# A projection's tile asks for the next two weight units, where it asked for the next one

## The chip, the core and the metric

The kernel runs on one core of a Trainium2 chip. A core has five engines that run side by side, each with its own queue, which it works through strictly in order: TensorE (PE, matrix products), VectorE (DVE), ScalarE (ACT), GpSimd (POOL) and SyncE (SP, which here only starts DMA transfers). An instruction that has to wait for another engine keeps back all that stands behind it on its own engine. The metric is the device time of one launch, in microseconds (us).

## What is computed

Two transformer blocks on 256 tokens of width 1024, in fp32. The first has an RWKV7 recurrence beside stick-breaking attention, then a feed-forward part. The second has a token mixer of two recurrences side by side and a mixture of 64 experts:

```python
def token_mixer(h, w_in, ...):
    proj = jnp.einsum('btd,de->bte', h, w_in)
    qkv = causal_short_conv(proj[..., :qkv_w], conv_w)
    ...
    oA = gated_delta_chunked(qA, kA, vA, g_log, beta)      # "gdn": a triangular solve per chunk of 64
    oA = rms_norm_2(oA, gdn_norm_w) * jax.nn.silu(gateA)
    ...
    oB = hgrn2_chunked(qB, kB, iB, logf)                   # "hgrn"
    oB = rms_norm_2(oB, hg_norm_w) * jax.nn.silu(gateB)
    return jnp.einsum('bte,ed->btd', jnp.concatenate([oA, oB], -1), w_out)
x = x + g1 * token_mixer(...)
x = x + g2 * moe(...)                                      # 64 experts, 8 for each token
```

## The kernel before, in words

**Weight units.** All projections outside the experts read one packed weight array, cut in 168 units of eight 128x128 tiles. `unit(u)` (L270) brings a unit in: SP loads it into one of three `raw` buffers (L274); ACT copies it, rounded to TensorE's fast fp32 format, into `whi` (L324); and DVE, or POOL for the thirty units listed in `POOLU`, writes the rest `wlo = raw - whi` (L325). `whi` and `wlo` have three buffers each. A tile then takes three matmuls (L330 to L332, L352 to L358): whi by the high part of x, whi by its low part, wlo by the high part; a unit is 24 matmuls. Most outputs (128 columns of a projection) take eight tiles, but since a block of twelve tiles stands early in the array, each output of the mixer takes the second half of one unit and the first half of the next.

**Asking ahead.** The line that the change is about is in `wt`, which every tile of a projection goes through:

```python
        hi, lo = self.unit(u)
        for v in range(u + 1, min(u + AHEAD + 1, -(-self.ntiles // UNIT) if u > 2 else 0)):
            self.unit(v)
```

So with `AHEAD = 1` the tile of unit u writes into the program the load and the split of unit u+1, if they are not there yet. Where these instructions then stand on each engine is settled by a scheduler, which orders the program by its own estimates; the strings `FIRST` and `MIXER` say in what order the program's streams (generators) are advanced.

**The mixer of the second block.** Its streams: `proj_fiq` (L1260 to L1281) makes hgrn's inputs: cumulated log decays by scans (L1270), queries (L1274), values (ACT copies, L1279). `proj_qv` makes gdn's queries and values, through `conv`: ACT takes the projection out of PSUM (L1130), DVE adds three shifted copies (L1133). `proj_gates2` (L1302) makes the gates. `gdn` builds the chunks' triangular matrices (masks on POOL, L1217 and L1218; product on DVE, L1223) and has `inverse` invert them: SP writes them to DRAM and back in another layout (L411, L414); `base_inverse` (L381) eliminates column by column on DVE, 31 pairs of a product (L393) and a subtraction (L394) on 32 partitions; ACT transposes (L395); SP writes the result to DRAM (`da`, L425) and reads it back (L429, L432); then PE goes on with products of small blocks (L403). `hgrn` works in two halves of 128 tokens: POOL copies inputs (L1409 to L1413), seven levels each take DVE differences (L1423, L1424), an exponential on ACT (L306), products on DVE and POOL (L1426, L1427), matmuls (L1429) and a masked copy on DVE (L1435). `second_mix` then makes the output projection, and the router and the experts follow, whose weights SP starts to load (L1729) behind the mixer's last `raw` loads.

Units 131 to 162 belong to this mixer: the first half of unit 143, whose `wlo` POOL makes, ends `proj_fiq`; its second half and the first of unit 144 make `proj_qv`'s first output; the gates end in the middle of unit 159, and the output projection begins there.

Of the kernel before, what the change touches and what calls it, by code (L numbers as in the profile page):

```python
# [40 lines left out]
UNIT = 8  # L41
RAW = 3
MIXER = 'kkkffkfkkfkfffffffkfqkkqqqqqqqqddghhfdhhgdhhgghhhhhhdhhhghh'
AHEAD = 1
POOLU = (17, 18, 26, 29, 36, 42, 46, 51, 65, 68, 69, 72, 94, 105, 109, 111, 112, 115, 116, 117, 119, 120, 121, 140, 143, 145, 149, 151, 158, 161)
NG = 12
FIRST = 'iiivvvivvvvvvsssssssswsssswgwxxwxxwxxxxwgwwwxgxxgooggggg'
# [162 lines left out]
class Ker:  # L210
# [74 lines left out]
    def wt(self, block, i):  # L285
        i += self.off[block]
        u = i // UNIT
# [3 lines that stand above are left out]
# [1889 lines left out]
```

## Time and profile before

| what | us |
| --- | --- |
| median of 3 runs | 1167.34 |
| lowest and highest of them | 1165.89, 1170.15 |
| the profiled execution's own time | 1175.33 |
| its span, from first to last instruction | 1173.5 |
| TensorE busy in it | 1086.6 |
| VectorE busy in it | 682.1 |
| ScalarE busy in it | 436.8 |
| GpSimd busy in it | 243.0 |

The rows come from the profiled execution, which took 8.0 us longer than the median of the runs; of its own time 1.83 us lie outside the span. Busy time is time in which an engine carries out instructions; the rest it waits. The stages follow each other in the trace: first block to about 360 us, its feed-forward part and the start of the second block to 556, the mixer from 556 to 732, router and experts from there to the end.

### The profile page before, as it was taken

To read this page: it belongs to the slowest core of one execution; us is meant where nothing else is said; L and a number is where in the kernel's file an instruction comes from. 1 tells how busy PE (TensorE), PEld (TensorE's weight loads), DVE (VectorE), ACT (ScalarE), POOL (GpSimd) and SP (SyncE) were. 2 spreads that over 40 slices of the span, in tenths; PEclk is the share of its full clock that TensorE was granted. 3 is DMA by queue.
4 is the path that set the end of the run, shared out by engine and by line. 5 is a ranking of instruction groups with operands and counts; after the bars stand their busy time and mean duration, and the time that the engine had idled before them with its cause. 6 is when DMAs were issued, how large, how long until landed. Compare 5 with 4: busy or idle time off the path is not lost.

```text
span 1173.5 us, 20361 instructions
## 1 busy us (share of the span) xinstructions
PE 1086.6 (93%) x8038; PEld 831.6 (71%) x8038; DVE 682.1 (58%) x1211; ACT 436.8 (37%) x707; POOL 243.0 (21%) x245
## 2 busy tenths in 40 slices
PE   5989899999989999988988999899999999999994
PEld 4889787789979999877988889773444444444441
DVE  5598633346678888877799888522233333333333
ACT  5744433365454444335854645411111111111112
POOL 1261102023312000486472131410000000000000
PEclk9899969999989999998999999799999999999998
DMA  5455511024558898864443504959999999999993
GB/s 174 141 145 176 177 55 37 1 86 166 179 198 298 314 341 302 306 232 145 148 146 127 176 28 174 415 182 344 418 413 392 419 419 419 399 419 418 420 418 139
DMA packets 67495, 290.69 MB, mean 248 GB/s; under 512 B 15984, under 2 KB 17136, under 8 KB 46912
## 3 DMA queue, kind: packets, MB, share of 16 engines
q1 hardware_dynamic: 66528, 287.93, 65.5%
q8 instruction: 66, 1.08, 0.4%
q10 hardware_dynamic: 864, 1.38, 0.3%
q14 instruction: 37, 0.30, 0.1%
HBM read 285.77 MB, written 3.51 MB: 247 GB/s over the span
## 4 chain that ended last, share of the span: by engine, by line
PE 45%; DMA 16%; DVE 11%; issue 4%; ACT 4%; POOL 3%; SPq 0%; POOLq 0%; ACTq 0%; DVEq 0%
DMA er<-in_E_dram 10%; PE bank L1880 10%; PE bank L1908 5%; PE p_b L357 3%; PE p_b L358 3%; PE p_b L352 3%; DMA wada<-in_W_ada_dram 3%; PE acc L1777 3%; PE bank L1840 3%; DMA xa<-in_E_dram 3%; DVE wada L1086 2%; DVE wlo L325 2%; PE p_b L787 2%; ACT k L306 2%; PE p_b L332 2%
## 5 line engine op out<-in xcount | busy, mean ns | idle before, releaser
L324 ACT ACTIVATE whi<-raw 128x1024 fp32r<-128x1024 f32 x168 | 175.5, 1055 | 102.7 <-PE p_b L331 37.0
L325 DVE TENSOR_TENSOR wlo<-raw,whi 128x1024 fp32r<-128x1024 f32 x138 | 178.4, 1299 | 59.5 <-ACT whi L324 55.4
L358 PE MATMUL p_b<-k,wlo 128*128 128x256 f32 x608 | 175.7, 290 | 4.9 <-DVE wlo L325 3.0
L352 PE MATMUL p_b<-k,whi 128*128 128x256 f32 x608 | 176.1, 290 | 3.5 <-ACT k L324 2.3
L357 PE MATMUL p_b<-k,whi 128*128 128x256 f32 x608 | 176.1, 290 | 2.3 <-DVE k L325 2.3
L332 PE MATMUL p_b<-k,wlo 128*128 128x256 f32 (+2 forms) x496 | 144.6, 296 | 13.1 <-DVE wlo L325 9.0
L330 PE MATMUL p_b<-k,whi 128*128 128x256 f32 (+2 forms) x496 | 146.8, 300 | 9.3 <-ACT k L324 4.1
L331 PE MATMUL p_b<-k,whi 128*128 128x256 f32 (+2 forms) x432 | 126.8, 296 | 0.3 <-DVE k L1114 0.3
L358 PEld LDWEIGHTS p_b<-k,wlo 128*128 128x128 f32 x608 | 118.6, 195 | 8.3 <-DVE wlo L325 4.0
L352 PEld LDWEIGHTS p_b<-k,whi 128*128 128x128 f32 x608 | 118.8, 196 | 5.1 <-ACT k L324 2.4
L325 POOL TENSOR_TENSOR wlo<-raw,whi 128x1024 fp32r<-128x1024 f32 x30 | 81.6, 2723 | 196.7 <-ACT whi L324 136.5
L357 PEld LDWEIGHTS p_b<-k,whi 128*128 128x128 f32 x608 | 118.8, 196 | 3.8 <-DVE k L325 2.8
L332 PEld LDWEIGHTS p_b<-k,wlo 128*128 128x128 f32 (+1 forms) x496 | 97.1, 198 | 15.8 <-DVE wlo L325 10.9
L330 PEld LDWEIGHTS p_b<-k,whi 128*128 128x128 f32 (+1 forms) x496 | 97.4, 198 | 14.6 <-ACT k L324 5.1
L1880 PE MATMUL bank<-er,x 128*32 128x512 f32 (+2 forms) x464 | 91.9, 612 | 2.6 <-DMA er<-in_E_dram 2.5
L1908 PE MATMUL bank<-er,k 128*32 128x512 f32 (+2 forms) x488 | 89.9, 595 | 2.6 <-DMA er<-in_E_dram 1.4
L1880 PE MATMUL bank<-er,h 128*32 128x512 f32 (+2 forms) x488 | 87.5, 595 | 0.0
L1828 POOL TENSOR_TENSOR k<-k,masks 128x128 f32<-128x128 f32 (+3 forms) x44 | 17.3, 423 | 335.7 <-DVE y L325 310.8
L331 PEld LDWEIGHTS p_b<-k,whi 128*128 128x128 f32 (+1 forms) x432 | 85.7, 199 | 0.8 <-DVE k L1114 0.6
L1086 DVE SCALAR_TENSOR_TENSOR wada<-wada,crow 128x1024 f32<-128x1024 f32 x48 | 70.9, 1484 | 21.7 <-DMA wada<-in_W_ada_dram 21.6
L1885 ACT ACTIVATE k<-bank 128x256 f32<-128x256 f32 x24 | 9.2, 384 | 195.7 <-PE bank L1880 195.7
L1886 DVE SCALAR_TENSOR_TENSOR k<-k,gs,bank 128x256 f32<-128x256 f32 x24 | 11.5, 481 | 101.9 <-ACT k L1885 101.9
(476 smaller groups left out, 2043.5 us busy)
## 6 DMA issues: line engine op xcount, KB each, us to landing
er<-in_E_dram SPq DMA_DIRECT2D x132, 1024.0 KB, 17.7
raw<-in_W_dram SPq DMA_DIRECT2D x168, 512.0 KB, 3.9
wada<-in_W_ada_dram SPq DMA_DIRECT2D x48, 512.0 KB, 5.5
xa<-in_E_dram SPq DMA_DIRECT2D x24, 1024.0 KB, 12.5
xa<-in_Sh_dram SPq DMA_DIRECT2D x2, 1024.0 KB, 8.3
k<-in_xT_dram SPq DMA_DIRECT2D x4, 272.0 KB, 4.7
dl<-x SPq DMA_DIRECT2D x1, 1024.0 KB
x<-in_xT_dram SPq DMA_DIRECT2D x1, 1024.0 KB
```

What stands on the lines that cost most here:

```text
L324: ins = self.nc.scalar.activation(hi, src, AF.Copy)
L325: (engine or self.nc.vector).tensor_tensor(lo, src, hi.bitcast(F32), op=OP.subtract)
L330: mm(out, w[0], x[0], start=start, stop=False)
L331: mm(out, w[0], x[1], start=False, stop=False)
L332: mm(out, w[1], x[0], start=False, stop=stop)
L352: a = mm(p[:, i], w[0], v[0], start=(n == 0), stop=False, **kw)
L357: mm(p[:, i], w[0], v[1], start=False, stop=False, **kw)
L358: mm(p[:, i], w[1], v[0], start=False, stop=last, **kw)
L1086: nc.vector.scalar_tensor_tensor(w, w, 1.0, c, op0=OP.mult, op1=OP.mult, accum_out=self.mod[:, o:o + 1])
L1777: self.nc.tensor.matmul(self.acc[t], w, x, start=t not in self.started, stop=False, skip_group_check=True)
L1880: mm(ph[t], X[:, k, i * 128 + t.start:i * 128 + t.stop], u[:, kk * 512:kk * 512 + 512], start=(k == 0), stop=(k == KD - 1), skip_group_che ...
L1908: nc.tensor.matmul(py[t], q.H[:, k, t], u[:, k * 1024 + c * 512:k * 1024 + c * 512 + 512], start=(k == 0), stop=(k == 1), skip_group_check ...
```

## The change

One constant is changed; nothing is computed in another way.

```diff
-AHEAD = 1
+AHEAD = 2
```

A tile of unit u now has the units u+1 and u+2 brought in. Each engine carries out the same instructions as before; what changes is the place of some of them, in the first block from unit 10 to 18 (44 to 90 us of the trace) and in the second block's mixer from unit 131 to 162 (556 to 720 us). Between these, units 19 to 130, each engine's order is the same as before.

On VectorE, where the mixer's triangular inverse begins. Before:

```order
L1426 TENSOR_TENSOR h_7056<-h_7056,h_7039 128x8x32
L1424 TENSOR_TENSOR h_7102<-h_7037 128x32x8
L1426 TENSOR_TENSOR h_7090<-h_7090,h_7039 128x16x16
L1426 TENSOR_TENSOR h_7102<-h_7102,h_7039 128x32x8
L393 TENSOR_TENSOR kt<-gate 32x31
L394 TENSOR_TENSOR gate<-gate,kt 32x31
```

and with the change:

```order
L325 TENSOR_TENSOR wlo<-raw,whi 128x1024
L1426 TENSOR_TENSOR h_7062<-h_7062,h_7045 128x8x32
L1426 TENSOR_TENSOR h_7096<-h_7096,h_7045 128x16x16
L1423 TENSOR_TENSOR h_7108<-h_7043 128x32x8
L1424 TENSOR_TENSOR h_7108<-h_7043 128x32x8
L1426 TENSOR_TENSOR h_7108<-h_7108,h_7045 128x32x8
L1133 SCALAR_TENSOR_TENSOR k_6553<-p_b_6555,cols,k_6553 128x255
L1133 SCALAR_TENSOR_TENSOR k_6553<-p_b_6555,cols,k_6553 128x254
L1133 SCALAR_TENSOR_TENSOR k_6553<-p_b_6555,cols,k_6553 128x253
L393 TENSOR_TENSOR kt<-gate 32x31
L394 TENSOR_TENSOR gate<-gate,kt 32x31
```

The `wlo` in the second piece is unit 144's, which stood inside the inverse before; the three L1133, which work on the product of units 143 and 144 (`p_b_6555`, `proj_qv`'s first output), stood behind the inverse's ninth pair and now stand ahead of its first.

On ScalarE, at the same place (the L1279 are `proj_fiq`'s last outputs, of which the last ends in unit 143; L1130 is `proj_qv`'s first). Before:

```order
L306 ACTIVATE h_7102<-h_7102 128x512
L1279 ACTIVATE k_5915<-p_b_6397 128x256
L1279 ACTIVATE k_5915<-p_b_6515 128x256
L324 ACTIVATE whi<-raw 128x1024 x3
L1130 ACTIVATE k_6547<-p_b_6549,cols 128x256
```

and with the change:

```order
L324 ACTIVATE whi<-raw 128x1024
L306 ACTIVATE h_7062<-h_7062 128x512
L1279 ACTIVATE k_5921<-p_b_6403 128x256
L306 ACTIVATE h_7096<-h_7096 128x512
L306 ACTIVATE h_7108<-h_7108 128x512
L1279 ACTIVATE k_5921<-p_b_6521 128x256
L1130 ACTIVATE k_6553<-p_b_6555,cols 128x256
```

Unit 144's `whi`, the first of the three behind the L1279 before, now stands ahead of three of hgrn's exponentials.

On SyncE, where the inverse's result is sent out. Before:

```order
L274 DMA raw<-in_W_dram 128x1024 x16
L425 DMA da_6505<-gate 32x1024 x2
L274 DMA raw<-in_W_dram 128x1024
L432 DMA gate<-da_6505 32x8x32
L429 DMA k_6429<-da_6505 32x8x32 x2
```

and with the change:

```order
L274 DMA raw<-in_W_dram 128x1024 x17
L425 DMA da_6511<-gate 32x1024 x2
L274 DMA raw<-in_W_dram 128x1024
L432 DMA gate<-da_6511 32x8x32
L429 DMA k_6435<-da_6511 32x8x32 x2
```

Since the loads' run begins one unit later than before (unit 145 instead of 144), it now ends with unit 161 instead of 159: units 160 and 161 are asked for ahead of `da`, and unit 162 in place of unit 160 between its writing and its reading. On POOL, the first of hgrn's copies (L1409) now stands ahead of the second pair of gdn's masks (L1217, L1218) instead of behind it.

## Rows read from the trace of the kernel before

**Rows 1.** The page's head: span, and busy time of each engine.
```profile
span 1173.5 us, 20361 instructions
PE 1086.6 (93%) x8038; PEld 831.6 (71%) x8038; DVE 682.1 (58%) x1211; ACT 436.8 (37%) x707; POOL 243.0 (21%) x245
```

**Rows 2.** The page's groups of `wlo`: count, busy us, mean ns, idle before.
```profile
L325 DVE TENSOR_TENSOR wlo<-raw,whi 128x1024 fp32r<-128x1024 f32 x138 | 178.4, 1299 | 59.5 <-ACT whi L324 55.4
L325 POOL TENSOR_TENSOR wlo<-raw,whi 128x1024 fp32r<-128x1024 f32 x30 | 81.6, 2723 | 196.7 <-ACT whi L324 136.5
```

**Rows 3.** Busy time by stage; the first line names the columns.
```profile
core 0: us, PE busy (x) PEld busy (x) DVE busy (x) ACT busy (x) POOL busy (x), PEclk, DMA share, GB/s
60.00:88.00 28.00, 24.80 (x205) 23.07 (x204) 27.30 (x37) 11.83 (x16) 17.73 (x14) 1.00 0.57 152
...
400.00:440.00 40.00, 39.77 (x335) 39.57 (x334) 36.37 (x55) 18.23 (x28) 2.40 (x1) 1.00 0.89 324
560.00:600.00 40.00, 36.86 (x297) 35.11 (x297) 31.96 (x63) 34.16 (x71) 20.53 (x22) 1.00 0.45 146
600.00:660.00 60.00, 51.23 (x396) 49.66 (x395) 58.98 (x121) 31.12 (x44) 19.65 (x11) 0.94 0.44 137
660.00:680.00 20.00, 19.54 (x219) 17.83 (x220) 15.21 (x21) 13.88 (x21) 6.80 (x5) 1.00 0.50 149
```

**Rows 4.** PE's waits in 556 to 730: us in total, times, longest.
```profile
PE p_b L332 <- DVE wlo L325: 4.1, 4, 2.5
PE p_b L332 <- POOL wlo L325: 4.0, 2, 2.4
PE p_b L358 <- DVE wlo L325: 1.7, 1, 1.7
```

**Rows 5.** DVE's timeline round the inverse: start, us, line; in brackets idle before.
```profile
604.18 0.42 DVE L1426 TENSOR_TENSOR h<-h,h 128x256 f32<-128x256 f32 x1 [0.36 <-ACT h L306]
604.52 0.19 DVE L393 TENSOR_TENSOR kt<-gate 32x31 f32<-32x31 f32 x1
...
605.23 2.33 DVE L394 TENSOR_TENSOR gate<-gate,kt 32x60 f32<-32x60 f32 x1
...
659.12 0.17 DVE L394 TENSOR_TENSOR gate<-gate,kt 32x31 f32<-32x31 f32 x1
```

**Rows 6.** Timelines of POOL, PE and ACT round units 143 and 144.
```profile
605.15 2.33 POOL L325 TENSOR_TENSOR wlo<-raw,whi 128x1024 fp32r<-128x1024 f32 x1
...
607.53 0.58 PE L332 MATMUL p_b<-k,wlo 128*128 128x256 f32 x1 [2.39 <-POOL wlo L325]
...
610.07 0.38 ACT L1279 ACTIVATE k<-p_b 128x256 f32<-128x256 f32 x1 [5.66 <-PE p_b L332]
...
614.20 0.48 ACT L1130 ACTIVATE k<-p_b,cols 128x256 f32<-128x256 f32 x1 [0.91 <-PE p_b L332]
```

**Rows 7.** DVE's groups inside the inverse, 604.5 to 659.4: busy us, mean ns.
```profile
L394 DVE TENSOR_TENSOR gate<-gate,kt 32x31 f32<-32x31 f32 (+15 forms) x31 | 18.8, 605 | 0.2
L325 DVE TENSOR_TENSOR wlo<-raw,whi 128x1024 fp32r<-128x1024 f32 x10 | 12.1, 1207 | 0.0
L1133 DVE SCALAR_TENSOR_TENSOR k<-p_b,cols,k 128x255 f32<-128x255 f32 (+2 forms) x24 | 11.1, 463 | 0.0
```

**Rows 8.** POOL's timeline ahead of unit 143's `wlo`.
```profile
591.05 1.69 POOL L1217 TENSOR_TENSOR k<-k,masks 128x512 f32<-128x512 f32 x1
592.70 1.68 POOL L1218 TENSOR_TENSOR k<-k,masks 128x512 f32<-128x512 f32 x1
596.61 0.61 POOL L1409 COPY h<-k 128x512 f32<-128x512 f32 x1 [2.23 <-DVE k L1270]
...
597.91 6.37 POOL L1413 COPY h<-k 128x512 f32<-128x512 f32 x1
```

**Rows 9.** Timelines of ACT, SP (its queue) and PE behind the inverse.
```profile
659.79 2.00 ACT L395 ACTIVATE gate<-gate 32x1024 f32<-32x1024 f32 x1
...
659.32 2.82 SPq L425 DMA_DIRECT2D da<-gate  x2
...
667.18 0.44 SPq L429 DMA_DIRECT2D k<-da  x1
...
669.19 0.69 PE L403 MATMUL p_b<-k,k 32*32 32x32 f32 x16
```

**Rows 10.** PE's timeline in the first block, unit 15.
```profile
81.28 0.39 PE L332 MATMUL p_b<-k,wlo 128*128 128x272 f32 x1 [1.54 <-DVE wlo L325]
```

## The prediction

> **What bounds the kernel now.** I read first the page's head: PE is busy 1086.6 of 1173.5 us, 93% [rows 1], which reads as a kernel bound by TensorE. That is an average over stages, so next I read the busy time by stage [rows 3]. In the feed-forward part (400 to 440) PE is busy 39.77 of 40 us and nothing ahead of it matters; there each engine's order is the same with the change, so that part gives nothing. The order differs in two places, and there the picture is another one. In the first block's 60 to 88, DVE is busy 27.30 of 28 us and PE 24.80. In the second block's mixer DVE is busy 58.98 of the 60 us from 600 to 660, with PE at 51.23, and in 660 to 680 PE is at 19.54 of 20.
>
> The third view is PE's waits in 556 to 730 [rows 4]: it waits for a `wlo` 4.1 + 4.0 + 1.7 = 9.8 us. This is what a reader would see first, a unit that comes too late, which asking earlier should mend. But PE waits there for DVE and for POOL, and of these DVE has no time left: no earlier request makes its 58.98 us of work shorter, it only puts `wlo` ahead of something else. So the question is what stands behind it on DVE, and the fourth view, DVE's timeline [rows 5], gives it: the base inverse, 62 small instructions from 604.52 to 659.29 (659.12 + 0.17), 54.8 us with other work between them. What comes after it is a chain in which each step waits for the one before: the transposition on ACT (659.79, 2.00 us), the writes of `da`, the reads back (the last at 667.18), the first L403 on PE at 669.19, 9.9 us after the inverse's end [rows 9]. The mixer's end hangs on this chain, and the experts' first weights are loaded behind the mixer's last units, so that a shift of the inverse's end comes through to the end of the kernel unless something in between takes it up.
>
> **The start of the inverse.** Before, the first L393 follows directly on the last of hgrn's L1426, at 604.52 [rows 5]. With the change three L1133 stand between them. They add up `proj_qv`'s first output, which takes the second half of unit 143 and the first half of unit 144 on PE, then the copy L1130 on ACT. Unit 144 is ready early now, since its `whi` and `wlo` have moved ahead. Unit 143 is not: its `wlo` is POOL's, done at 605.15 + 2.33 = 607.5, and PE waited 2.39 us for it and went on at 607.53 [rows 6]. On POOL it has the same instructions ahead of it as before, so I keep 607.5. From there, PE's rest of unit 143's first half ends with the ACT copy that it releases at 610.07 [rows 6], 2.5 us; the output behind it is 24 matmuls. Their pace is 119 ns in 400 to 440 (40 us by 335 matmuls) [rows 3]: 2.9 us, and some 0.3 us more because the first of them run at the slower pace that holds until 610.4 (the stage's granted clock is 0.94 [rows 3]). So PE has the output at about 613.2; before it was there at 614.20, when ACT started L1130, because PE waited for unit 144 as well [rows 6]. Then 0.48 for L1130 [rows 6] and 3 x 0.463 = 1.4 for the three L1133 [rows 7]: the inverse starts at 613.2 + 0.5 + 1.4 = 615.1, that is **10.6 us later**. DVE's queue stands still for most of that, for it is in order and the units behind the inverse cannot pass.
>
> **Its length.** Inside it, before, stood 24 L1133 and ten `wlo` [rows 7]. By the order, 21 L1133 stand there with the change (3 x 0.463 = 1.4 us less), unit 144's `wlo` has left and unit 157's has come (0), and two gate products of about the price of an L1133 have come (0.9 more): 0.5 us less. The second L394 took 2.33 us, from 605.23, while POOL's `wlo` of unit 143 ran, from 605.15 for the same 2.33 [rows 5, 6]; the mean of the 31 is 0.605 [rows 7], and in a quieter place it would be some 0.3. With the change DVE waits while that `wlo` runs, and 2.0 us are saved. The inverse's end is thus at +10.6 - 0.5 - 2.0 = **+8.1 us**.
>
> The Trainium skill (SBUF — State Buffer, "Who interferes with whom") says that a VectorE instruction with two inputs in SBUF and a GpSimd instruction that reads SBUF shut each other out for a whole instruction. By that rule the 2.33 us are a lock and leave with the collision; were they due to the instruction itself, they would stay, and this term would be +10.1.
>
> **The bounds of the start.** POOL's `wlo` may move. Ahead of it stands the copy L1413, which took 6.37 us where the copy L1409 of the same shape took 0.61 [rows 8], while DVE worked without a gap: if DVE's new waits let it through, 5.7 us leave. On the other side, L1409 now stands ahead of gdn's second pair of masks (1.69 + 1.68 [rows 8]) and waits for the scans; the masks, and L1223, L1274 and L1413 behind them, can come up to 2.7 us later (L1409 at 596.61, its 0.61 and the masks' 3.4 behind it give 600.6 for L1413's start in place of 597.91). So the inverse's end lies between +2.4 and +10.8; I take the middle row's +8.1, because DVE's queue round L1413 holds the same work as before.
>
> **Behind the inverse.** In 660 to 680 PE was full (19.54 of 20) with the gates' units beside the chain, and DVE at 15.21 [rows 3]. With the inverse late, PE does these units while it waits, and the chain then meets an emptier PE; DVE has a `wlo` less to make behind the inverse (1.2 [rows 7]) and a pair of gate products. This gives back between 0 and 5 us (5 is a quarter of those 20 us, in which the chain's small products and the gates' matmuls share PE); I take 2.5. On SP, units 160 and 161 now stand ahead of the writes of `da` and unit 162 ahead of its reading. An issue costs about as much as the L429's, 0.44 [rows 9]; each has to wait until the unit three before it is split. The `wlo` of 157 stands on DVE within the inverse, ahead of its end, so the loads are past when `da` comes: 0 for the sum, +1 as its upper bound, and more only in the rival below.
>
> **The first block.** PE waited 1.54 us for unit 15's `wlo` [rows 10]; that `wlo` comes earlier, but DVE is full there (27.30 of 28 [rows 3]) and the work that it gives way to is waited for a few us later. Between -1.6 (all of it) and +0.5; I take 0.
>
> **The sum.** +8.1 - 2.5 + 0 + 0 = +5.6 us against the profiled execution's 1175.33. That execution was 8.0 us above the median of 1167.34, so I put the difference on the median: 1172.9.
>
> **The rivals.** (a) The delay passes as worked out, with the term behind the inverse between 0 and 5: +3.1 to +8.1, 1170.4 to 1175.4. This is my forecast. (b) POOL's copy gets through: +2.4 - 2.5 = -0.1, 1167.2. For it: 6.37 against 0.61 [rows 8]. Against it: DVE has no fewer two-input instructions there. (c) Faster: PE is what the mixer's end waits for, as the 93% and the 19.54 of 20 suggest, and the delay of the inverse is covered by the PE work that is done meanwhile. Then what counts is PE's waits: 9.8 us less the 2.4 for unit 143's `wlo`, which stay [rows 4]: -7.4, 1159.9. It decides if the inverse's delay is below what the chain behind it has to spare, that is, if L403 could start late by it without PE running dry; the 9.9 us in which the chain waits for ACT and DMA speak against it, since PE has no part in them. The Trainium skill (Trainium Kernel Development and Optimization, "Best Practices") advises to double-buffer, so that loads overlap with computing; followed one unit further it speaks for this case. (d) Slower by more: the masks' slip of 2.7 us comes on top, and a load ahead of `da` waits for a `wlo` on POOL (unit 158's, 2.7 us [rows 2]): +5.6 + 2.7 + 2.7 = +11.0, 1178.3. (e) The change does nothing: with three buffers a third unit can only be split once the first is used up, and where DVE is full the scheduler's places mean little: 1167.3.
>
> **How the numbers follow.** What a measurement of this kernel can tell from no change is about 0.5%, 5.8 us; above 1173.2 is slower, below 1161.5 faster. Case (a) has 0.50, and its span lies half below and half above 1173.2: 0.26 and 0.24. Case (b) has 0.12 and (e) 0.08, both within. Case (c) has 0.13, faster. Case (d) has 0.17, slower. Faster 0.13, same 0.46, slower 0.41. The range has to leave out no more than 0.2: it leaves out (c) and the top of (d): 1164 to 1179.
>
> **What would show it.** In the profile with the change: DVE's first L393 near 615 (in (b) near 609) with a wait of DVE for ACT's L1130 or PE ahead of three L1133; no 2.3 us L394; the inverse's end near 667; the waits of PE for `wlo` in 556 to 730 down from 9.8 to 2 to 4 us, with a new wait of PE later for the chain (L403 or what follows); SP's `da` writes right behind the inverse, not behind a load. I am wrong if the first L393 stays near 604.5, if the mixer's end moves by another amount than the inverse's end less 0 to 5 us, or if the difference lies in the first block.

## The result and the profile after

The changed kernel takes 1182.08 us (median of 4 runs, 1179.04 to 1183.19), beside 1168.74 for the kernel before (median of 4, 1165.89 to 1172.12, of which the forecast had three, with 1167.34 as their median). The ratio is 1.010, with a 95% interval of 1.0072 to 1.0127: 8 to 15 us slower, clear of no change. The forecast was 1172.9 in a range of 1164 to 1179, which ends 3 us short; "slower" had 0.41 in it, behind "same" with 0.46. The medians further down leave out two single executions, one of e7 and one of e10, that lay more than 1.5% above the fastest of their kernel.

TensorE's waits for `wlo`, which a reader would have wanted gone, did shrink, though not to the 2 to 4 us of the forecast: the waits in 553 to 740 (us in total, times, longest) show 3.4 + 2.9 = 6.3 us where [rows 4] had 9.8. Others have come:

```profile
PE p_b L1429 <- POOL h L1427: 5.2, 2, 4.5
PE p_b L332 <- DVE wlo L325: 3.4, 2, 3.0
PE p_b L332 <- POOL wlo L325: 2.9, 2, 1.6
PE p_b L330 <- DVE k L1274: 2.4, 1, 2.4
```

The busy time by stage (columns as in [rows 3]) shows where:

```profile
core 0: us, PE busy (x) PEld busy (x) DVE busy (x) ACT busy (x) POOL busy (x), PEclk, DMA share, GB/s
560.00:600.00 40.00, 36.20 (x294) 34.66 (x294) 30.09 (x60) 33.85 (x70) 19.19 (x21) 1.00 0.40 144
600.00:660.00 60.00, 50.14 (x403) 48.94 (x402) 58.21 (x112) 31.50 (x42) 15.35 (x9) 0.97 0.43 139
660.00:680.00 20.00, 15.04 (x158) 14.22 (x158) 11.26 (x28) 11.27 (x16) 7.27 (x5) 0.83 0.47 144
```

From 600 to 660 DVE is as full as before. From 660 to 680, where PE was busy 19.54 us [rows 3], it is busy 15.04, at a granted clock of 0.83 of full speed instead of 1.00, and DVE 11.26 instead of 15.21. Both wait.

**Where to measure from.** The spans, 1179.9 and 1173.5, differ by only 6.4 us, half of what the medians differ by. The profiled execution of before was one of the longer ones, and the mixer does not begin at one time: the first L1114 (the mixer's norm) starts at 545.93 in the profile of before, and at 538.59 in that of the fourth experiment below, whose program is the same up to there. So the stages are compared from the first L1114 on. The mixer's end is that of the last L1392, the output projection's matmuls; in the profile of before these marks stand at 545.9 and 741.7, somewhat wider than the 556 to 732 given further up. The table gives, from the timelines' starts and ends, how long each stretch took in us, and in the last column how much of the mixer PE waited (the stretch less PE's busy time in it). The inverse begins where its first L393 starts to run.

| kernel | L1114 to end of last L1274 | to first L393 | to inverse's end | to first L403 | to mixer's end | mixer, sum | PE's waits in it |
| --- | --- | --- | --- | --- | --- | --- | --- |
| before | 51.9 | 6.7 | 54.8 | 9.9 | 72.5 | 195.8 | 15.3 |
| after | 53.3 | 13.0 | 52.7 | 12.6 | 74.2 | 205.8 | 23.2 |
| units below 60 alone (e1) | 52.5 | 6.7 | 54.6 | 10.0 | 72.5 | 196.3 | 14.9 |
| units 140 to 149 alone (e3) | 51.9 | 16.0 | 50.0 | 10.7 | 74.7 | 203.3 | 23.6 |
| the same, taps behind (e9) | 52.6 | 10.6 | 55.3 | 9.1 | 71.9 | 199.5 | 14.7 |
| units 150 on alone (e4) | 52.1 | 6.7 | 58.3 | 13.6 | 71.5 | 202.1 | 19.4 |
| after, taps behind (e5) | 54.8 | 11.3 | 51.8 | 14.5 | 72.7 | 205.1 | 21.2 |
| below 150, taps behind (e13) | 54.1 | 11.5 | 51.4 | 8.9 | 71.8 | 197.8 | 15.2 |

("Taps" are the three L1133 of `proj_qv`'s first output.) The mixer has become 10.0 us longer, which agrees with the interval of the runs: 5.6 us up to the inverse's end and 4.4 behind it. PE carries out the same matmuls in every row, so a longer mixer is more waiting of PE or longer busy time: of the 10.0 us, 7.9 are waits (23.2 instead of 15.3) and 2.1 busy time, at a mean granted clock of 0.96 of full speed instead of 0.97. The inverse's end, counted from the first L1114, is a worse guide than these waits: it is late by 5.6 us in the changed kernel and by 3.7 to 5.2 in e3, e4, e5, e9 and e13, and yet e9 and e13, in which PE waits no longer than before, lose little.

**The start of the inverse** is late, but not by the wait that was forecast. DVE's timeline in the changed kernel (start, us; idle before in brackets), lines left out:

```profile
598.81 2.62 DVE L1423 TENSOR_TENSOR h<-h 128x256 f32<-128x256 f32 x1
601.36 0.96 DVE L1424 TENSOR_TENSOR h<-h 128x256 f32<-128x256 f32 x1
...
603.24 1.76 DVE L325 TENSOR_TENSOR wlo<-raw,whi 128x1024 fp32r<-128x1024 f32 x1
...
607.59 0.43 DVE L1426 TENSOR_TENSOR h<-h,h 128x256 f32<-128x256 f32 x1 [0.70 <-ACT h L306]
608.23 1.52 DVE L1133 SCALAR_TENSOR_TENSOR k<-p_b,cols,k 128x255 f32<-128x255 f32 x3 [0.21 <-ACT k L1130]
609.66 1.97 DVE L393 TENSOR_TENSOR kt<-gate 32x31 f32<-32x31 f32 x1
```

and POOL's:

```profile
596.73 0.75 POOL L1413 COPY h<-k 128x512 f32<-128x512 f32 x1 [0.76 <-DVE k L1274]
597.43 0.95 POOL L405 MEMSET k<- 128x1024 f32 x1
598.53 2.62 POOL L325 TENSOR_TENSOR wlo<-raw,whi 128x1024 fp32r<-128x1024 f32 x1 [0.15 <-ACT whi L324]
```

The L1133 wait 0.21 us. POOL's copy L1413, 6.37 us before [rows 8], takes 0.75, and unit 143's `wlo` is done at 601.15 instead of 607.5. What POOL gains, DVE pays: its L1423 starts at 598.81 while that `wlo` runs, and takes 2.62 us where the next one takes 0.41. Such lengthened instructions between L1274 and L393 sum to some 4.3 us (each over the usual duration of its shape), the L1133 with their wait to 1.7, and the wait for ACT is 0.3 longer: together the 6.3 us that the gap has grown by. Unit 144's `wlo` has come in, and that of unit 141 has gone ahead of L1274, which cancel.

**Behind the inverse**, the queue of SP and PE's timeline:

```profile
656.00 4.28 SPq L274 DMA_DIRECT2D raw<-in_W_dram  x3
662.42 2.35 SPq L425 DMA_DIRECT2D da<-gate  x2
...
669.67 0.45 SPq L429 DMA_DIRECT2D k<-da  x1
```

```profile
665.18 3.78 PE L1429 MATMUL p_b<-h 128*128 128x128 f32 x16 [4.49 <-POOL h L1427]
...
674.99 0.69 PE L403 MATMUL p_b<-k,k 32*32 32x32 f32 x16
```

`da` starts 0.03 us behind the inverse's end (DVE's last L394, 662.22 + 0.17): the loads ahead of it keep nothing back here. The last reading of `da` is issued at 669.67, and in the profile of before L403 followed 2.0 us behind that issue [rows 9]; here it follows 5.3 behind. PE got to an L1429 of hgrn at 660.7, waited 4.49 us for POOL's L1427, and had the gates' units 157 (second half) to 159 still to do, 47 matmuls that stand behind the L1429 and ahead of the L403. In the profile of before, the gates' last 18 matmuls stood between and behind the L403, and PE waited only 0.55 us between the inverse's end and the first L403.

The wait costs more than its own length. PE in three stretches of the changed kernel (columns as above):

```profile
660.70:665.18 4.48, 0.00 (x0) 0.00 (x0) 4.04 (x13) 3.40 (x5) 3.05 (x2) 0.78 0.52 164
665.18:670.00 4.82, 4.82 (x22) 4.82 (x23) 2.26 (x5) 1.91 (x4) 1.74 (x2) 0.50 0.66 172
670.00:675.00 5.00, 5.00 (x44) 4.86 (x42) 1.71 (x3) 2.12 (x2) 0.14 (x1) 1.00 0.25 66
```

After 4.48 us in which PE did nothing, it ran at a granted clock of 0.50 for 4.82 us and got 22 matmuls done; the next 5.00 us, at 1.00, hold 44. At that pace the 22 would have taken 2.5 us, so by this estimate the clock costs 2.3 us, as much again as the wait itself adds behind the inverse's end (2.8 us instead of 0.55). Against the two stand 15 matmuls fewer ahead of L403, and in sum L403 comes 2.7 us later behind the inverse's end (12.6 instead of 9.9). The other 1.7 of the 4.4 us lie behind L403, where PE waits 4.8 us in place of 2.7.

### The profile page after: what moved, and what is told of

Read it like the earlier page. It is cut to its first block, busy times and chain, and to the rows that moved or that the text cites. A ratio compares the mean times of both kernels' runs of the same rounds, so it can differ in the third digit from the quotient of the medians.

```text
span 1179.9 us, 20366 instructions
## 1 busy us (share of the span) xinstructions
PE 1086.5 (92%) x8038; PEld 829.1 (70%) x8038; DVE 679.3 (58%) x1211; ACT 437.1 (37%) x707; POOL 238.5 (20%) x245
## 4 chain that ended last, share of the span: by engine, by line
PE 51%; DMA 21%; DVE 16%; ACT 4%; issue 4%; POOL 3%; SPq 0%; ACTq 0%; POOLq 0%; DVEq 0%
DMA er<-in_E_dram 10%; PE bank L1880 9%; DMA wada<-in_W_ada_dram 7%; PE bank L1908 4%; DVE wlo L325 4%; PE p_b L330 3%; PE p_b L331 3%; PE p_b L332 3%; PE acc L1777 3%; PE bank L1840 3%; DVE wada L1086 3%; DMA xa<-in_E_dram 3%; PE p_b L358 2%; PE p_b L357 2%; PE p_b L352 2%
## 5 line engine op out<-in xcount | busy, mean ns | idle before, releaser
L325 POOL TENSOR_TENSOR wlo<-raw,whi 128x1024 fp32r<-128x1024 f32 x30 | 78.9, 2637 | 213.5 <-ACT whi L324 213.0
L332 PEld LDWEIGHTS p_b<-k,wlo 128*128 128x128 f32 (+1 forms) x496 | 96.5, 196 | 11.5 <-DVE wlo L325 8.2
L1886 DVE SCALAR_TENSOR_TENSOR k<-k,gs,bank 128x256 f32<-128x256 f32 x24 | 11.5, 481 | 101.7 <-ACT k L1885 101.7
```

Of the source, the lines that this page charges most:

```text
L325: (engine or self.nc.vector).tensor_tensor(lo, src, hi.bitcast(F32), op=OP.subtract)
L332: mm(out, w[1], x[0], start=False, stop=stop)
```

## Experiments

The times are medians; each group of runs was compared with runs of the kernel before on the same chip, whose single executions reach from 1163 to 1179, so the ratios' intervals carry the verdicts. That kernel's median was 1170 to 1173 in these groups, 2 to 4 us above the 1168.7 from which the expectations were reckoned; so a difference from it is compared with what an expectation gives over 1168.7. The first four split the change by units.

**e1, units below 60 alone.**

```diff
-        for v in range(u + 1, min(u + AHEAD + 1, ...
+        for v in range(u + 1, min(u + (2 if u < 60 else AHEAD) + 1, ...
```

> Two units ahead only for units below 60, so only the first block's order differs from before. Theory 'mixer' (the whole loss of 13.3 us comes from the second block's mixer): 1168.7 within 3 us, or up to 3 us faster, since the trace with the change ran the first block's units 14 to 73 some 2 to 5 us earlier than the trace of before. Rival 'first block' (the traces' stages mislead, and a part of the loss is made there): 1172 or more.

1172.32 beside 1172.13, ratio 0.9999 (0.9973 to 1.0025). The first block neither gains nor loses; PE's 1.54 us there [rows 10] are worth nothing that can be measured. So the 2 to 5 us by which the trace with the change had been earlier there are put down to scatter.

**e2, units from 126 on alone.**

```diff
-        for v in range(u + 1, min(u + AHEAD + 1, ...
+        for v in range(u + 1, min(u + (2 if u > 125 else AHEAD) + 1, ...
```

> Two units ahead only from unit 126 on; the mixer's order is the changed kernel's word for word, the first block's that of before. Theory 'mixer': 1182 to 1185, at least as slow as the whole change. Rival 'first block': below 1179, with the rest found in the run of the first block alone.

1181.81 beside 1172.13, ratio 1.0089 (1.0055 to 1.0124); mixer 204.6 us. The whole loss is the mixer's.

**e3, units 140 to 149 alone.**

```diff
-        for v in range(u + 1, min(u + AHEAD + 1, ...
+        for v in range(u + 1, min(u + (2 if 140 <= u < 150 else AHEAD) + 1, ...
```

> Two units ahead for units 140 to 149 alone. VectorE's three L1133 stand ahead of the first L393 as in the changed kernel, while SyncE's loads stand behind the writes of da as before, and hgrn's L1429 of the level behind the inverse stand where they stood before on TensorE. Theory 'start' (the late start of the inverse is the loss, and it passes whole): first L393 5 us later than before, 1174 to 1179. Theory 'behind' (most is lost behind the inverse, by the order of TensorE and the loads): the inverse 5 us later but the time within 1169 to 1172, because the chain behind takes it up.

1181.26 beside 1172.13, ratio 1.0082 (1.0047 to 1.0118): 9.1 us, at the upper end of what the theory "start" gave, and nearly all of the change's loss. Here POOL's order is that of before, and the wait that was forecast stands in the trace. DVE, POOL and ACT:

```profile
604.51 0.43 DVE L1426 TENSOR_TENSOR h<-h,h 128x256 f32<-128x256 f32 x1 [0.36 <-ACT h L306]
605.73 3.17 DVE L325 TENSOR_TENSOR wlo<-raw,whi 128x1024 fp32r<-128x1024 f32 x1 [0.79 <-ACT whi L324]
612.72 1.52 DVE L1133 SCALAR_TENSOR_TENSOR k<-p_b,cols,k 128x255 f32<-128x255 f32 x3 [3.82 <-ACT k L1130]
614.15 1.97 DVE L393 TENSOR_TENSOR kt<-gate 32x31 f32<-32x31 f32 x1
```

```profile
598.25 6.38 POOL L1413 COPY h<-k 128x512 f32<-128x512 f32 x1
604.57 0.95 POOL L405 MEMSET k<- 128x1024 f32 x1
605.48 2.33 POOL L325 TENSOR_TENSOR wlo<-raw,whi 128x1024 fp32r<-128x1024 f32 x1
```

```profile
612.21 0.48 ACT L1130 ACTIVATE k<-p_b,cols 128x256 f32<-128x256 f32 x1 [2.47 <-PE p_b L332]
```

POOL ends unit 143's `wlo` at 607.8, ACT gets the output at 612.21, DVE stands still for 3.82 us in front of the L1133, and the inverse starts 16.0 us behind L1274 instead of 6.7. It is 4.7 us shorter then (fewer L1133 inside, fewer lengthened instructions), so that it ends 4.6 us late; what stands behind it adds 3.0 us, where the theories had it add nothing or take some back.

**e4, units from 150 on alone.**

```diff
-        for v in range(u + 1, min(u + AHEAD + 1, ...
+        for v in range(u + 1, min(u + (2 if u >= 150 else AHEAD) + 1, ...
```

> Two units ahead from unit 150 on alone. The inverse begins as before; behind it one load stands ahead of the writes of da, hgrn's L1429 stand 26 matmuls later on TensorE, and the first L403 stands behind unit 159's matmuls. Theory 'start': 1168 to 1170. Theory 'behind': 1172 to 1176, with L403 3 us or more later against the inverse's end than the 9.9 us of before.

1177.97 beside 1172.13, ratio 1.0066 (1.0036 to 1.0097): 5.8 us, as the theory "behind" has it. The inverse starts as before, but is 3.5 us longer, since unit 157's `wlo`, two gate products and one more L394 of 2.3 us (beside POOL's `wlo` of unit 158) fall into it. L403 follows its end at 13.6 us. DVE, SP and PE:

```profile
655.42 0.17 DVE L394 TENSOR_TENSOR gate<-gate,kt 32x31 f32<-32x31 f32 x1
```

```profile
655.63 2.37 SPq L425 DMA_DIRECT2D da<-gate  x2
```

```profile
659.27 3.78 PE L1429 MATMUL p_b<-h 128*128 128x128 f32 x16 [3.91 <-POOL h L1427]
669.18 0.50 PE L403 MATMUL p_b<-k,k 32*32 32x32 f32 x10
```

It is the changed kernel's picture: `da` goes out at once, PE waits 3.9 us in front of an L1429, works off the gates' units, and takes L403 late. So the two parts lose 9.1 and 5.8 us singly and 9.7 together (e2); they do not add up. That one's delay hides in the other's is a reading that no run shows by itself.

**e5, the changed kernel with the taps behind again.** The three L1133 get one ordering, behind the inverse's ninth pair, as the order of before had them:

```diff
@@ base_inverse
-            nc.vector.tensor_tensor(M[:, c:, :c], M[:, c:, :c], u, op=OP.subtract)
+            i = nc.vector.tensor_tensor(M[:, c:, :c], M[:, c:, :c], u, op=OP.subtract); self.inv = i if j <= 8 else self.inv
@@ conv
-            nc.vector.scalar_tensor_tensor(dst[:, j, d:], ...)
+            i = nc.vector.scalar_tensor_tensor(dst[:, j, d:], ...); c == 0 and self.order(i, self.inv)
```

> The changed kernel with one ordering added: the three L1133 of the first output of proj_qv stand behind the inverse's ninth pair, as before the change, while unit 144's wlo and all else stay early. Theory of the prediction (the inverse starts late because it stands behind these L1133 and what they wait for): the first L393 5 us or more earlier against L1274's end than the changed kernel's 13.0 us, and a time of 1175 to 1178. Rival 'shared work' (in the changed kernel's trace POOL's wlo of unit 143 was done long before, the L1133 cost only their own 1.7 us, and the other 4.3 us of the late start are instructions of DVE drawn out while POOL works): first L393 1 to 2 us earlier, the 1.4 us come back inside the inverse, time within 2 us of the changed kernel, 1180 to 1184.

1180.16 beside 1170.74, ratio 1.0094 (1.006 to 1.0128): no gain that can be told from the changed kernel. The rival is right about the start, 11.3 us instead of 13.0 behind L1274, though not that the 1.4 us come back inside the inverse, which is 0.9 us shorter. So the inverse ends 1.1 us earlier (117.8 instead of 119.0 behind the first L1114), and another wait comes out from under it. DVE, SP and POOL:

```profile
656.14 0.17 DVE L394 TENSOR_TENSOR gate<-gate,kt 32x31 f32<-32x31 f32 x1
```

```profile
652.97 7.29 SPq L274 DMA_DIRECT2D raw<-in_W_dram  x3
660.32 0.88 SPq L425 DMA_DIRECT2D da<-gate  x2
```

```profile
655.66 4.24 POOL L325 TENSOR_TENSOR wlo<-raw,whi 128x1024 fp32r<-128x1024 f32 x1 [27.35 <-ACT whi L324]
```

The inverse ends at 656.3, `da` goes out at 660.3. The load of unit 161 stands ahead of it and needs the buffer of unit 158, whose `wlo` POOL ends at 659.9. This is case (d)'s load, 4.0 us; in the changed kernel POOL ended that `wlo` at 659.93, and the inverse, which ended at 662.39, covered it.

**e6, the gates ahead of hgrn's levels on TensorE.** In `MIXER`, two `g` move ahead of two `h`:

```diff
-MIXER = 'kkkffkfkkfkfffffffkfqkkqqqqqqqqddghhfdhhgdhhgghhhhhhdhhhghh'
+MIXER = 'kkkffkfkkfkfffffffkfqkkqqqqqqqqddghhfdhhgdgghhhhhhhhdhhhghh'
```

> The changed kernel with two letters of MIXER moved, so that the gates' last units, 157 to 159, stand on TensorE ahead of hgrn's L1429 of the two levels behind the inverse instead of behind them; start and length of the inverse and SyncE's order are the changed kernel's. Theory 'TensorE's queue' (behind the inverse the loss is L403 standing behind units that stand behind an L1429 which waits 4.5 us for POOL's L1427): L403 at 9.5 to 10.5 us behind the inverse's end instead of 12.6, and 2 to 4 us faster than the changed kernel, 1178 to 1181. Rival 'loads' (SyncE's three loads round da are the loss): L403 as late as before, no change, 1182.

1187.99 beside 1170.74, ratio 1.0125 (1.0077 to 1.0174): no gain on the changed kernel, and rather a loss, so the theory in this form falls. PE's timeline:

```profile
667.15 1.13 PE L1429 MATMUL p_b<-h 128*128 128x128 f32 x8 [2.28 <-DVE h L1426]
...
670.73 3.36 PE L1429 MATMUL p_b<-h 128*128 128x128 f32 x14 [2.45 <-POOL h L1427]
674.02 1.06 PE L403 MATMUL p_b<-k,k 32*32 32x32 f32 x16
```

The units run early, and L403 now stands directly behind the L1429, which wait themselves: 12.9 us behind the inverse. In this order, too, PE stands still while hgrn's level passes through DVE, ACT and POOL.

**e7, both edits.** The diffs of e5 and e6 together, on the changed kernel.

> Both of the last two edits on the changed kernel: the three L1133 behind the ninth pair and the gates ahead of hgrn's levels. If the two add up: the sum of their gains against the changed kernel, 1174 to 1180; if the late start comes from work that POOL and DVE keep from each other, only the gates' part, 1178 to 1181. Faster than the kernel before only if both theories are too small.

1184.99 beside 1170.74, ratio 1.0115 (1.0071 to 1.0159). Nothing adds up to a gain; both expectations were too low.

**e8, unit 143's `wlo` on DVE.**

```diff
-POOLU = (..., 140, 143, 145, ...)
+POOLU = (..., 140, 145, ...)
```

> The changed kernel with unit 143's wlo on DVE instead of POOL; the order of TensorE is the changed kernel's. DVE gets one wlo more, 1.2 us, ahead of the inverse, and POOL none beside hgrn's first level. Theory 'shared work': the L1423 that took 2.62 us beside POOL's wlo falls to 0.4, the first L393 comes 1 to 2 us earlier than in the changed kernel against L1274's end, total 0 to 3 us faster, 1179 to 1182. Rival (the 2.62 us have another cause, and DVE only gets work added): first L393 1 us later, 1183.

1182.59 beside 1170.74, ratio 1.0103 (1.007 to 1.0135). The L1423 that took 2.62 us is down to at most 0.96, and the lengthening between L1274 and L393 from 4.3 to 2.1 us. It shows that POOL's `wlo` lengthened it. But DVE has 1.2 us more to do and waits 1.20 us for ACT's L1130 in place of 0.21, so L393 comes only 0.3 us earlier, and `da` waits 3.0 us for the loads, as in the fifth.

**e9, the third with the taps behind.** The diffs of e3 and e5 together.

> The run with two units ahead for 140 to 149 alone, with the three L1133 put back behind the inverse's ninth pair; unit 144's wlo stays early, POOL and nearly all of SyncE stand as before the change. Theory 'start': the gap between L1274's end and the first L393 falls from 15.6 us to 7 to 9 (6.3 before, and unit 144's wlo, 1.2), and 5 to 8 us of that run's loss go, 1171 to 1175. Rival (the loss there is not the wait ahead of the L1133): 1178 or more.

1173.10 beside 1170.33, ratio 1.0028 (1.0005 to 1.0051): of 9.1 us all but 2.8 are gone. With the third run this is the cleanest pair of the study: the place of the taps alone differs. The gap ahead of L393 falls from 16.0 to 10.6 us, less than the 7 to 9 expected. DVE's timeline:

```profile
603.20 0.42 DVE L1426 TENSOR_TENSOR h<-h,h 128x256 f32<-128x256 f32 x1 [0.37 <-ACT h L306]
604.41 3.16 DVE L325 TENSOR_TENSOR wlo<-raw,whi 128x1024 fp32r<-128x1024 f32 x1 [0.80 <-ACT whi L324]
607.50 0.71 DVE L393 TENSOR_TENSOR kt<-gate 32x31 f32<-32x31 f32 x1
```

What is left of the gap, 4.0 us over the 6.7 of before, is unit 144's early `wlo`, 3.16 us beside POOL's instead of 1.2, and its wait of 0.80 for ACT.

But the time was not won where the theory looked for it. The inverse starts 5.3 us earlier and is 5.3 us longer (DVE waits 3.9 us inside it instead of 0.6), so it ends no earlier than in the third run: 118.5 us behind the first L1114, beside 117.9. The gain lies behind the inverse, where the rest of the mixer takes 81.0 us instead of 85.4 and PE waits 2.5 us instead of 6.5. The taps' place costs its time there; through which instruction, these two traces do not show.

**e10, taps behind and loads behind.** The diff of e5, and the loads of units 160 on ordered behind `da`:

```diff
-            nc.sync.dma_start(raw, self.ins["W"][u])
+            d = nc.sync.dma_start(raw, self.ins["W"][u]); u >= 160 and self.order(d, self.sent)
```

(`self.sent` is the L425 transfer.)

> The changed kernel with the three L1133 behind the ninth pair, as in the run with that alone, and with the loads of units 160 on ordered behind the writes of da. With that one edit alone the writes of da started 4.0 us behind the inverse's end (660.32 against 656.32). Theory 'loads' (a raw buffer that POOL's wlo of unit 158 still held kept them back): da starts at the inverse's end, L403 follows 3 to 4 us earlier than in that run against the inverse's end (14.5 there), 1176 to 1179. Rival (TensorE's queue is later anyway): L403 as late as 14 us behind the inverse, 1180 to 1184.

1185.01 beside 1170.33, ratio 1.0131 (1.0093 to 1.017). The writes of `da` do start at the inverse's end now (658.52 against 658.50), and L403 still comes 13.9 us behind it, in which PE waits 3.07 us for an L1427: the rival's answer. Later, the stretch from L467 to the last L1463 takes 38.2 us instead of the changed kernel's 33.2; that the late loads are missed there is a guess, since the mixer as a whole is no more than 0.9 us longer than in the fifth (205.9 and 205.1).

**e11, three undone**, the tenth with the gates' units 158 and 159 ordered behind the first L403, and **e12**, only that ordering on the changed kernel:

```diff
-            a = mm(p[:, i], w[0], v[0], start=(n == 0), stop=False, **kw)
+            a = mm(p[:, i], ...); block == 'gates2' and (self.off[block] + m * kt + k) // UNIT >= 158 and self.order(a, self.l403)
```

> The last kernel, and the gates' units 158 and 159 behind the first L403 on TensorE. If start, loads and TensorE's queue are the whole loss: L403 at 9 to 10.5 us behind the inverse's end, and 1170 to 1175, near the kernel before. If shared work of DVE and POOL ahead of the inverse is a part of its own, some 4 us of it stay: 1175 to 1179.

> The changed kernel with only the gates' units 158 and 159 put behind the first L403 on TensorE. Theory 'TensorE's queue': L403 at 9 to 10.5 us behind the inverse's end instead of 12.6, 2 to 3 us faster than the changed kernel, 1178 to 1181. Rival (what L403 gains, the gates lose, and the mixer's end waits for them as well): L403 early, the time not, 1182 or more.

1190.21 and 1195.51 beside 1170.33, ratios 1.018 (1.0148 to 1.0211) and 1.0222 (1.0195 to 1.025). L403 gains little in the twelfth (11.9 us behind the inverse), and from L467 to the last L1463 it takes 41.5 us instead of the changed kernel's 33.2. The rival is right about the time: what is put behind L403 delays what follows. The scheduler also moves other work when one instruction is tied down, so these two tell about their own order more than about the changed kernel's.

**e13, units below 150 with the taps behind.** All of the change up to unit 149, first block included, with the diff of e5.

```diff
-        for v in range(u + 1, min(u + AHEAD + 1, ...
+        for v in range(u + 1, min(u + (1 if u >= 150 else 2) + 1, ...
```

> Two units ahead for all units below 150 (the first block's and the mixer's up to there), one from 150 on, and the three L1133 behind the inverse's ninth pair. Theory 'requests from 150 on' (the longer tail is theirs): inverse's end to mixer's end 81 to 83 us as before the change (82.4), and what is left is DVE's and POOL's shared work ahead of the inverse, 2 to 5 us: 1173 to 1176. Rival: the tail stays at 85 or more, 1178 to 1182.

1173.92 beside 1173.09, ratio 1.0028 (0.9997 to 1.0058), within noise of no change. DVE, SP and PE:

```profile
656.77 0.72 DVE L394 TENSOR_TENSOR gate<-gate,kt 32x31 f32<-32x31 f32 x1
```

```profile
657.52 2.44 SPq L425 DMA_DIRECT2D da<-gate  x2
```

```profile
666.43 0.69 PE L403 MATMUL p_b<-k,k 32*32 32x32 f32 x16
```

L403 comes 8.9 us behind the inverse's end, and the part behind it is 80.7 us where before it was 82.4 and in the changed kernel 86.8. Set beside the others, this settles what the loss hangs on. With the taps ahead of the inverse and no early requests from unit 150 on, it stays (e3, ratio 1.0082); with those requests and the taps behind, it stays (e5, 1.0094); with neither, it is gone but for a rest within or near the noise (e13 and e9, 1.0028 each). The part behind the inverse goes the same way: 85.4 us, 87.2, and 80.7 and 81.0. Either of the two is enough for most of the loss.

**e14, the loads behind `da` and nothing else.** The diff of e10 alone, on the changed kernel.

> The changed kernel with only SyncE's loads of units 160 on ordered behind the writes of da. In the changed kernel's trace these writes start at the inverse's very end (662.42 against 662.39), so the loads keep nothing back there: no change, 1180 to 1184, if that reading holds. Rival 'loads' (they delay the chain all the same, by the reads behind): 2 to 4 us faster, 1178 to 1180.

1181.98 beside 1173.09, ratio 1.0107 (1.0061 to 1.0153). No change that can be told: in the changed kernel as it is, SP's loads cost nothing that shows in the time.

No version beat the kernel before.

## Why the prediction was wrong, step by step

**What bounds the kernel: right about `wlo`, too simple about the inverse.** The waits for `wlo` were no measure of the loss. They shrank by 3.5 us and the mixer grew by 10.0. But "a shift of the inverse's end comes through to the end of the kernel unless something in between takes it up" does not describe what was met: in e9 the inverse ends 0.6 us later than in e3, counted from the first L1114, and the mixer is 3.8 us shorter. All of PE's waits together follow the loss better than that end, and it is these waits that have to be forecast.

**The start of the inverse: the mechanism right, its place in this kernel half wrong.** "On POOL it has the same instructions ahead of it as before, so I keep 607.5" is the sentence that failed. The instructions were the same, but L1413 met DVE at another moment and went through in 0.75 us instead of 6.37, and unit 143's `wlo` was there at 601.15. That is case (b), which had 0.12. Its benefit did not arrive: the time that POOL no longer lost, DVE lost (4.3 us of lengthened instructions), and with the L1133 the start came 6.3 us later against L1274, 7.7 against the mixer's start. The forecast was 10.6; with POOL's order of before, in e3, it is 9.3, and DVE's wait for the L1133 is there.

The bounds for (b) moved POOL's copy and left DVE's instructions at their price of before. The Trainium skill (SBUF — State Buffer, "Who interferes with whom") says that whichever of two such instructions issues first holds the shared ports for its whole length. The rows agree: DVE's L1423 starts inside POOL's `wlo` and ends 0.3 us behind it, and in e8, with that `wlo` gone from POOL, it is short. The collision that was avoided at one place was met at the next here.

**The length: the number right, the reason not.** -2.5 us were forecast and -2.0 measured. The forecast counted on one collision less, that of an L394 with unit 143's `wlo`. As many pair instructions of about 2 us stand in the inverse as before, four, each beside a `wlo` of POOL; the fourth is now beside unit 158's:

```profile
657.81 2.23 DVE L393 TENSOR_TENSOR kt<-gate 32x87 f32<-32x87 f32 x1
```

What did leave are four pair instructions that were 0.4 us too long each beside POOL's L1427, which now end before the inverse. That this comes to about the same sum is luck.

**Behind the inverse: wrong, and this is the step that failed.** It was sized at -2.5 us, between -5 and 0, and measured +4.4; the prediction's own sign of being wrong, a mixer's end that moves by more than the inverse's end, is met (10.0 and 5.6 us). "With the inverse late, PE does these units while it waits, and the chain then meets an emptier PE" came true in its first half: at the inverse's end the traces have 48 of the gates' matmuls left, where before it was 77. The second half overlooks that PE's queue is in order too: the units that were left stand behind hgrn's L1429, and this one waits for POOL's L1427, which begins at 662.13, when DVE is only just finishing the inverse. PE stood for 4.49 us with work behind it whose weights were ready (unit 158's `wlo` was done at 659.93, unit 159's at 663.87), and then ran at half its clock. From the inverse's end to the mixer's, PE has 32 matmuls fewer to do than before (652 instead of 684) and is busy as long, 79.2 us each time, since the granted clock is 0.94 instead of 1.00; and it waits 7.6 us instead of 3.2. So what the emptier queue gave, the clock took, and the new waits are the 4.4 us. The bound "at most 0" had no row behind it. In e9 and e13, where PE waits 2.5 us behind the inverse and its clock there is 1.00, the part does give back 1.5 and 1.7 us. Why PE meets those waits in one order and not in another stays open in part: every order that was forced there singly (e6, e10, e12) made another wait.

**SP's loads: right for the changed kernel** (e14), but by luck of timing: they cost 4.0 us in e5, where the inverse ends earlier. Case (d) had a wait that is real, but not in this kernel; that its time, 1178.3, is the nearest of all is luck too.

**The first block: right**, 0 (e1).

**The sum.** Against +5.6 stand 10.0 us in the traces from the mixer's start: start and length together +5.6 instead of +8.1, the part behind +4.4 instead of -2.5. The 4.4 us that are missing are half of what the forecast is short of the measured time (1182.08 less 1172.9, 9.2 us). The other half is the base: the forecast stood on 1167.34, the median of three runs, and in the larger groups the same kernel had 1170.3 to 1173.1. Either error alone would have left the time inside the range (1167.34 + 10.0 is 1177.3). Case (c), faster by 7.4 us since PE would no longer wait, is refuted by e2 and e3; its premise, that the mixer's time follows PE's waits, fits the table, but it looked only at the waits that would go and not at those that would come.

## What to carry to other kernels

In a stage where an engine is full, an earlier request made nothing shorter here; ask which chain its instructions are moved ahead of, and follow that chain's first instruction on each in-order queue. When a chain is delayed, work that could fill the gap only does so if it stands ahead of the next waiting instruction in its own queue, so read that queue in the new order before writing down a gain, and give TensorE's new waits a price beyond their length where the trace shows a lower clock behind them. Compare the stretches of two profiles from a common mark, and look where a gain lies before saying what made it: in e9 the start that was mended gained nothing at the inverse's end. And undo parts in pairs: here the taps ahead of the inverse and the early requests from unit 150 on each cost most of the loss alone, so that undoing one of them gained nothing (e5) and undoing both took it away (e13).

## What the runs showed of the hardware

The same POOL copy of 128x512 took 6.37 us in one order and 0.75 us in the other, and the same DVE difference of 128x256 took 0.41 us, or 2.62 beside POOL's `wlo`. Which of the two engines pays changed with a shift of a few us, and 2 to 4 us moved with it. Behind its longest wait PE also ran slower: after 4.48 us without a matmul the granted clock was 0.50, the lower of its two levels (1.2 and 2.4 GHz), for 4.82 us, in which 22 matmuls ran; then it was 1.00 again, and 44 ran in 5.00 us. In the kernel before, with PE busy for 19.54 of the 20 us from 660 to 680, it was 1.00 throughout [rows 3].
